# The up products of a gated MLP by Strassen's seven block products, with the residual kept in DRAM

## The chip, the cores and the metric

The kernel runs on one core of one Trainium2 chip. The metric is the device time of one execution in microseconds (us). A core has TensorE (PE in the profile; its weight loads are PEld), VectorE (DVE), ScalarE (ACT), GpSimd (POOL) and SyncE (SP), which here issues nearly all DMA transfers. On-chip memory is SBUF, with 128 partitions; matmuls write to PSUM, eight banks of 128 x 512 float32.

## The reference

Two decoder layers over 1024 tokens of width 1024: first a gated DeltaNet mixer, then sliding-window attention. After the mixer each layer has a gated MLP with a causal depthwise convolution, then a small gated embedding; one RMSNorm closes. The change concerns the MLP:

```python
def conv_ffn(x, w_up, conv_w, w_down):          # D_FF = 2816, three taps
    u = causal_dwconv(x @ w_up, conv_w)         # x: 1024 tokens x 1024
    gate, val = u[..., :D_FF], u[..., D_FF:]
    return (jax.nn.silu(gate) * val) @ w_down

h = h + mix
h = h + conv_ffn(rmsnorm(h, norm_ffn[i]), f_w_up[i], f_conv[i], f_w_down[i])
```

## The kernel before

Channels lie on the partitions and tokens along the free axis, so that a tile is 128 channels x 1024 tokens. Every float32 product is made of three passes: an operand is split into a high part in the matmul's own format (fp32r) and a low part, the rest; high by high, high by low and low by high are added up in PSUM. Weights come from DRAM tile by tile (`load_w`: the DMA, the high part on ACT at line 192, the low part on POOL at line 193). Activations are split once, the high part on ACT and the low part on DVE (lines 236 and 237, with the norm's weight multiplied in).

The mixer's output projection ends in `OutProj.finish`: per tile of the residual `hT[m]` 18 matmuls, two additions from PSUM (line 837), then `Norm.add`, which splits the tile and adds its square to a running sum (lines 255, 256). The norm's factor for a token is multiplied in later, on the way out of PSUM.

The MLP (`ffn`) has 22 pairs of a gate tile and a value tile. `up(j)` makes both: two weight tiles, each by all eight channel tiles and both halves of the tokens, 2 x 2 x 8 x 3 = 96 matmuls of 512 columns. Each half leaves PSUM by one DVE multiplication (line 292). The convolution is one ACT pass (line 295) and two DVE passes (line 297) for a tile. Then come silu on ACT, gate times value on DVE (line 1133), and the split of the product, ACT and POOL (lines 231, 232). `down` multiplies two to four finished pairs at a time into all eight residual tiles and adds 16 PSUM halves to `hT`, which stays in SBUF (line 1166); for one pair this is 48 matmuls on average. So one pair costs TensorE 144 matmuls of 512 columns.

What sets the order: a scheduler places each engine's instructions by its own estimates, and each engine then runs its list strictly in that order. In parts where `E.pinned` is set, TensorE keeps the order in which the program is written; in the MLP it is not set before, and is set after. Buffers are fixed tiles: 40 slots of 4 KB per partition (`Slots`, reused oldest first), weight buffers in rings (`wraw`, `whi`, `wlo`, three of each), and PSUM rings `mm` (3 banks), `d` (3) and `s` (2). Waits arise where a ring or slot is not yet free.

Of the kernel before, what the change touches and what calls it, by code (L numbers as in the profile page):

```python
# [8 lines left out]
F32 = mybir.dt.float32  # L9
# [29 lines left out]
# matmul passes of the running product put between the steps of a chain:  # L39
# DeltaNet's decay, its heads' preparation, inverses, scan, the last scan; attention  # L40
# [7 lines left out]
GROUPS = [2, 4, 4, 4, 4, 4]  # L48


class Slots:
    """Hands out the fixed 4 KB tiles; a tile given back is reused oldest first."""
# [6 lines left out]
    def get(self, name, dt=F32, w=T):  # L59
        self.free.sort()  # L60
        i = self.free.pop(0)[1]
        self.n += 1
        t = self.pool.tile([P, w], dt, tag=f"S{i}", name=f"{name}_{self.n}")
        return Slot(t, i)

    def put(self, *ts):
        for t in ts:
            self.free.append((self.n, t.i))

# [33 lines left out]
def kernel(  # L103
# [36 lines left out]
    class PE:  # L140
        """TensorE; while pinned is set its instructions keep the order they are written in"""
# [54 lines left out]
    def passes(ps, wh, wl, xs, h, k0=0):  # L196
        """a product's matmuls, one a step"""
# [18 lines left out]
    def proj(src, xs, bank=None):  # L216
        """[128 outputs, T] in two PSUM tiles."""
# [8 lines left out]
    def split(t, name, scale=None, eng=V, parts=1):  # L226
        """float32 tile -> two float32r tiles whose sum it is (times scale)."""
# [13 lines left out]
    class Norm:  # L241
        """RMSNorm over channels, tile by tile: the weight goes onto the
        tiles, the per-token factor comes as a row tile at the end."""
# [32 lines left out]
        def rows(self):  # L276
            """the factor along the tokens, on every partition"""
# [4 lines left out]

    def spread(dst, r):
        """a column of each 128 tokens -> a row on every partition"""
# [3 lines left out]
        A.copy(dst, pb)  # L288
# [11 lines left out]
    def delta_layer():  # L300
# [21 lines left out]
        # TensorE is warm by the time the first tile is there  # L322
# [76 lines left out]
        # a chunk's matrix takes P more than its P * P elements, so that the  # L399
# [418 lines left out]
    class OutProj:  # L818
# [36 lines left out]
        def finish(self, nxt):  # L855
# [6 lines left out]
            for a, b in xs:  # L862
                S.put(a, b)
# [528 lines left out]
```

## Time and profile before

| | us |
|---|---|
| time, median of 3 runs | 2845.87 |
| the runs | 2845.24 to 2848.56 |
| span of the profiled execution | 2841.9 |
| PE busy | 2757.3 (97%) |
| DVE busy | 1362.0 (48%) |
| ACT busy | 940.2 (33%) |
| POOL busy | 944.9 (33%) |
| MLP of layer 0, by its first and last adds | about 743 to 1480 |
| MLP of layer 1 | about 1972 to 2716 |

The span runs from the first to the last instruction on the core. The page gives no time of its own for the profiled execution; the median lies 3.97 us above its span. Busy shares are means over stages of different kinds, and a busy matmul is counted from its issue to the end of its pipeline, so neighbours overlap. The rows used below are in a section of their own.

### The profile page before, as it was taken

Reading aid. Unit: us, or ns where it says so; the run is one execution under the profiler, and the core shown is the slowest. Engines: PE = TensorE matmul, PEld = TensorE weight load, DVE = VectorE, ACT = ScalarE, POOL = GpSimd, SP = SyncE. Lnnn points to the kernel's source line nnn. Section 1 sums busy time; section 2 is a strip of 40 time slices with the busy share of each in tenths; the row PEclk is TensorE's granted clock in tenths of the full one; section 3 lists DMA queues with packets and bytes.
Section 4 is the critical chain, followed back from the end, with each engine's and each line's share of the span. In section 5 each row is a group of like instructions: output and inputs, shape, how many; then the busy total and the mean of one; then the engine's idle time right before and its main releaser. Section 6 shows DMA issues by size and latency. Waiting matters only on the chain. (4 is left out here: it accounts for less than half of the span.)

```text
span 2841.9 us, 33819 instructions
## 1 busy us (share of the span) xinstructions
PE 2757.3 (97%) x13442; PEld 2233.0 (79%) x13442; DVE 1362.0 (48%) x1885; ACT 940.2 (33%) x1696; POOL 944.9 (33%) x850
## 2 busy tenths in 40 slices
PE   8999999999999999999999998999999999999998
PEld 7777887878888888888878776678888888888786
DVE  6455455564644343434354346654542434343555
ACT  5333343342422121212243235643321212121343
POOL 4444343341332333223232322222323322323344
PEclk9999999999999999999999999999999999999998
DMA  4222121231120211111112211221111020111123
GB/s 160 86 70 70 55 68 48 57 108 47 54 63 27 65 30 66 30 64 35 58 58 77 88 56 42 54 68 61 44 44 60 30 67 27 63 30 60 51 88 107
DMA packets 111758, 172.95 MB, mean 61 GB/s; under 512 B 32752, under 2 KB 68976, under 8 KB 111600
## 3 DMA queue, kind: packets, MB, share of 16 engines
q1 hardware_dynamic: 110736, 169.41, 19.3%
q8 instruction: 106, 1.74, 0.2%
q10 hardware_dynamic: 864, 1.38, 0.1%
q14 instruction: 52, 0.43, 0.0%
HBM read 148.67 MB, written 15.79 MB: 58 GB/s over the span
## 5 line engine op out<-in xcount | busy, mean ns | idle before, releaser
L193 POOL TENSOR_TENSOR wlo<-wraw,whi 128x1024 fp32r<-128x1024 f32 (+4 forms) x306 | 567.6, 1856 | 1197.2 <-ACT whi L192 1175.0
L146 PE MATMUL mm<-xh,whi 128*128 128x512 f32 x1560 | 634.9, 407 | 1.1 <-DVE gt L292 1.0
L146 PE MATMUL mm<-xh,wlo 128*128 128x512 f32 x1560 | 626.6, 402 | 1.0 <-POOL wlo L193 0.9
L146 PE MATMUL mm<-xl,whi 128*128 128x512 f32 x1560 | 623.5, 400 | 2.4 <-DVE xl L237 2.4
L192 ACT CAST whi<-wraw 128x1024 fp32r<-128x1024 f32 (+4 forms) x306 | 247.1, 808 | 1013.2 <-PE d L146 766.9
L146 PEld LDWEIGHTS mm<-xh,wlo 128*128 128x128 f32 x1560 | 295.6, 189 | 67.0 <-POOL wlo L193 1.8
L146 PEld LDWEIGHTS mm<-xl,whi 128*128 128x128 f32 x1560 | 295.8, 190 | 60.6 <-DVE xl L237 3.6
L146 PEld LDWEIGHTS mm<-xh,whi 128*128 128x128 f32 x1560 | 295.5, 189 | 58.2 <-issue 2.2
L297 DVE SCALAR_TENSOR_TENSOR yf<-zf,fcv,yf 128x1024 f32<-128x1024 f32 x176 | 284.2, 1618 | 109.4 <-ACT yf L295 106.5
L146 PE MATMUL d<-xh,whi 128*128 128x512 f32 x808 | 319.2, 395 | 0.0
L146 PE MATMUL d<-xh,wlo 128*128 128x512 f32 x808 | 319.0, 395 | 0.0
L146 PE MATMUL d<-xl,whi 128*128 128x512 f32 x808 | 318.7, 394 | 0.0
L292 DVE TENSOR_TENSOR zf<-d,rb 128x512 f32<-128x512 f32 x88 | 60.9, 692 | 373.1 <-PE d L146 373.1
L146 PEld LDWEIGHTS d<-xh,wlo 128*128 128x128 f32 x808 | 151.9, 188 | 36.4
L146 PEld LDWEIGHTS d<-xl,whi 128*128 128x128 f32 x808 | 151.6, 188 | 36.4
L146 PEld LDWEIGHTS d<-xh,whi 128*128 128x128 f32 x808 | 151.7, 188 | 35.6
L146 PE MATMUL mm<-gh,wlo 128*128 128x512 f32 x352 | 138.8, 394 | 3.1 <-POOL wlo L193 3.1
L232 POOL TENSOR_TENSOR gl<-yf,gh 128x1024 fp32r<-128x1024 f32 x44 | 105.8, 2404 | 104.6 <-ACT gh L231 104.4
L146 PE MATMUL mm<-gh,whi 128*128 128x512 f32 x352 | 138.7, 394 | 0.0
L146 PE MATMUL mm<-gl,whi 128*128 128x512 f32 x352 | 138.7, 394 | 0.0
L146 PE MATMUL d<-gh,wlo 128*128 128x512 f32 x352 | 138.6, 394 | 0.0
L146 PE MATMUL d<-gl,whi 128*128 128x512 f32 x352 | 138.5, 394 | 0.0
(291 smaller groups left out, 4113.5 us busy)
## 6 DMA issues: line engine op xcount, KB each, us to landing
wraw<-f_up SPq DMA_DIRECT2D x88, 512.0 KB, 3.4
wraw<-f_down SPq DMA_DIRECT2D x80, 256.0 KB, 2.6
wraw<-a_in SPq DMA_DIRECT2D x32, 512.0 KB, 3.5
wraw<-g_w SPq DMA_DIRECT2D x24, 512.0 KB, 3.4
row<-rowd SPq DMA_DIRECT2D x16, 512.0 KB, 4.3
wraw<-b_in SPq DMA_DIRECT2D x12, 512.0 KB, 3.6
ad<-A SPq DMA_DIRECT2D x8, 512.0 KB, 3.2
X<-xd SPq DMA_DIRECT2D x8, 512.0 KB, 4.4
```

What stands on the lines that cost most here:

```text
L146: i = nc.tensor.matmul(*a, **k)
L192: A.copy(hi, raw)
L193: G.tensor_tensor(lo, raw, hi[:, :].bitcast(F32), SUB)
L232: eng.tensor_tensor(lo[:, :], t[:, 0:T], hi.f(), SUB)
L292: V.tensor_tensor(dst[:, off + h * 512:off + (h + 1) * 512], ps2[h], rb[:, hs(h)], MUL)
L297: V.scalar_tensor_tensor(dst[:, 0:T], z[:, i:i + T], w[:, i:i + 1], dst[:, 0:T], MUL, ADD)
```

## The change

Strassen's scheme (in Winograd's form). Rows of the block matrix are gate and value, the inner dimension is split into even and odd channel tiles, and the tokens into their two halves. Seven block products of 4 x 3 = 12 matmuls take the place of eight: 84 matmuls instead of 96 for a pair. For this

- the activations become seven sets, `b11`, `b21`, `b22` (blocks as they are) and `t1` to `t4` (sums of blocks), each in high and low parts. They are made by `Mix.add`, tile by tile, at the end of the mixer's output projection, in place of `Norm.add`;
- three further sums and one more of the weight blocks are made on DVE for each pair (`weights`), and all seven weight blocks are split in pieces of 512 columns, four products ahead (`AHEAD`);
- the products are combined on DVE on their way out of PSUM; three banks (`p1`, `p7`, `p5`) take two products each. The norm's factors stay in the two `s` banks. Nine DVE instructions of 512 columns take the place of four;
- the residual `h` goes to DRAM (`hf`) and is read and written again for each `step` of the down products. A step is one output tile by two pairs, 12 matmuls; up to four steps stand between the up products of a pair. Before, a down product took four pairs for most groups. The last four pairs are taken as before, with `h` loaded back;
- the split of gate times value has its low part on DVE instead of POOL; convolution inputs use two fixed tiles (`S.wide`) instead of slots.

```diff
 class OutProj
-        def finish(self, nxt):
+        def finish(self, nxt, l):
             xs = self.parts(NP1, KT)
-            nrm = Norm(nxt)
-            fx = []
+            mix = Mix(nxt, l)
             for m in range(KT):
                 self.add(m, xs, NP1)
-                fx.append(nrm.add(self.h[m]))
...
+                mix.add(m, self.h[m])
+            return mix
+    class Mix:
...
+        def pair(self, t, name, names, eng):
...
+            for h in range(2):
+                A.copy(hi[:, hs(h)], t[:, hs(h)])
+                eng.tensor_tensor(lo[:, hs(h)], t[:, hs(h)], hi[:, hs(h)].bitcast(F32), SUB)
...
+        def add(self, m, t):
+            nc.sync.dma_start(self.hf[m], t[:, 0:T])
+            xw = S.get("xw")
+            for h in range(2):
+                A.activation(xw[:, hs(h)], t[:, hs(h)], AF.Copy, scale=self.nrm.w[:, m:m + 1])
+            a, b = hs(0), hs(1)
+            if m % 2 == 0:
+                self.t12 = S.get("t12")
+                V.tensor_tensor(self.t12[:, a], xw[:, a], xw[:, b], SUB)
+                bb = S.get("b11", F32R)
+                A.copy(bb[:, a], xw[:, a])
+                V.tensor_tensor(bb[:, b], xw[:, a], bb[:, a].bitcast(F32), SUB)
...
+            else:
+                t12, x0 = self.t12, self.xw
+                V.tensor_tensor(t12[:, b], xw[:, b], t12[:, a], ADD)
+                self.pair(t12, "t12", ("t1", "t2"), V)
+                t34 = S.get("t34")
+                V.tensor_tensor(t34[:, a], x0[:, b], xw[:, b], SUB)
+                V.tensor_tensor(t34[:, b], xw[:, a], t12[:, b], SUB)
+                S.put(t12, x0)
+                self.pair(t34, "t34", ("t3", "t4"), G)
+                S.put(t34)
+                self.pair(xw, "x1", ("b21", "b22"), G)
+                S.put(xw)
+            self.nrm.square(t)
+            S.put(t)
...
+        def halves(src):
...
+            A.copy(hi, src)
+            G.tensor_tensor(lo, src, hi.bitcast(F32), SUB)
+            return hi, lo
...
+        def weights():
...
+                yield halves(a11)
+                V.tensor_tensor(s1, a21, a22, ADD)
+                V.tensor_tensor(s2, s1, a11, ADD)
+                yield halves(s2)
+                V.tensor_tensor(s3, a11, a21, ADD)
+                yield halves(s3)
+                yield halves(s1)
+                yield halves(a12)
+                yield halves(a22)
+                V.tensor_tensor(s2, s2, a12, ADD)
...
+                yield halves(s2)
...
+        def load_step():
...
+            nc.sync.dma_start(w, f_down[l, m, :, a * P:(a + 2) * P])
...
+            nc.sync.dma_start(t[:, 0:T], hf[m])
+            A.copy(hi, w)
+            G.tensor_tensor(lo, w, hi[:, :].bitcast(F32), SUB)
...
+        def step():
+            a, m, hi, lo, t = loaded.pop(0)
+            load_step()
+            xs = [gs[a], gs[a + 1]]
+            for h in range(2):
+                ps = pdt()
+                mm3(ps, hi, lo, xs, h)
+                V.tensor_tensor(t[:, hs(h)], t[:, hs(h)], ps, ADD)
+            nc.sync.dma_start(hf[m], t[:, 0:T])
...
+        def up(j, early, late):
...
+            if j == 0:
+                w = take(4)
+                ps = [pmt(), pdt(), pmt(), pmt()]
+                for k in range(KT // 2):
+                    for p, v, xn in zip(ps, w, ("b11", "t2", "t3", "t1")):
+                        prod(p, v, xn, (k,))
...
+            else:
+                p1 = pmt()
+                prod(p1, *take(), "b11")
+                A.copy(dd, p1)
+                for _ in range(early[0]):
+                    step()
+                p6 = pdt()
+                prod(p6, *take(), "t2")
+                V.tensor_tensor(dd, p6, dd, SUB)
+                for _ in range(early[1]):
+                    step()
+                gated(j - 1)
+                p7 = pmt()
+                prod(p7, *take(), "t3")
+                V.tensor_tensor(zh(z2, 1), p7, dd, ADD)
+                p5 = pmt()
+                prod(p5, *take(), "t1")
+                V.tensor_tensor(zh(z2, 1), zh(z2, 1), p5, SUB)
+                V.tensor_tensor(zh(z2, 1), zh(z2, 1), rb[1], MUL)
...
+            prod(p1, *take(), "b21", first=False)
...
+                A.copy(zh(z1, 0), p1)
+                V.tensor_tensor(zh(z1, 0), zh(z1, 0), rb[0], MUL)
+                prod(p7, *take(), "t4", first=False)
...
+            V.tensor_tensor(zh(z2, 0), p7, dd, ADD)
+            V.tensor_tensor(zh(z2, 0), zh(z2, 0), rb[0], MUL)
+            for _ in range(late[0]):
+                step()
+            ys[j] = taps(2 * j + 1, z2)
+            prod(p5, *take(), "b22", first=False)
...
+            V.tensor_tensor(zh(z1, 1), p5, dd, SUB)
+            V.tensor_tensor(zh(z1, 1), zh(z1, 1), rb[1], MUL)
+            for _ in range(late[1]):
+                step()
```

The scheduler's order shows in three places. First TensorE where the MLP of layer 0 begins. Before, the first two products take the eight split tiles (`xh`, `xl`) in turn:

```order
L146 MATMUL mm<-xh_6032,whi 128x512
L146 MATMUL mm<-xl_6033,whi 128x512
L146 MATMUL mm<-xh_6032,wlo 128x512
L146 MATMUL d<-xh_5789,whi 128x512
L146 MATMUL d<-xl_5790,whi 128x512
L146 MATMUL d<-xh_5789,wlo 128x512
```

After, the last matmul of the output projection (`oh`, `ol`) is followed by the first four products in turn, three matmuls each (`b` is `b11`, the first `t12h` is `t2`, `t34h` is `t3`, the second `t12h` is `t1`):

```order
L152 MATMUL mm<-oh_5756,wlo 128x512
L152 MATMUL mm<-b_197_5796,whi 128x512 x2
L152 MATMUL mm<-b_197_5796,wlo 128x512
L152 MATMUL d<-t12h_5833,whi 128x512
L152 MATMUL d<-t12l_5834,whi 128x512
L152 MATMUL d<-t12h_5833,wlo 128x512
L152 MATMUL mm<-t34h_5842,whi 128x512
L152 MATMUL mm<-t34l_5843,whi 128x512
L152 MATMUL mm<-t34h_5842,wlo 128x512
L152 MATMUL mm<-t12h_5833,whi 128x512
```

So the fourth matmul of the MLP already needs the weights of a second block.

Second, POOL at the same place. Before, it has only the low parts of weights there (128x384 for the output projection):

```order
L193 TENSOR_TENSOR wlo<-wraw,whi 128x640
L193 TENSOR_TENSOR wlo<-wraw,whi 128x384 x2
L779 TENSOR_TENSOR f<-f,mhalf 128x8
L193 TENSOR_TENSOR wlo<-wraw,whi 128x384
L1125 MEMSET zf_6179 128x2
L193 TENSOR_TENSOR wlo<-wraw,whi 128x384 x4
```

After, the low parts of `b21` and `b22` (`x1l`) and of `t3` and `t4` (`t34l`) stand between them, and the low parts of the summed weights (from `sa`, `sb`) behind them:

```order
L199 TENSOR_TENSOR wlo<-wraw,whi 128x384 x2
L898 TENSOR_TENSOR x1l_5946<-xw_5926,x1h_5945 128x512 x2
L898 TENSOR_TENSOR t34l_5940<-t_214_5936,t34h_5939 128x512 x2
L199 TENSOR_TENSOR wlo<-wraw,whi 128x384 x2
L898 TENSOR_TENSOR x1l_6043<-xw_6023,x1h_6042 128x512
L1193 TENSOR_TENSOR wlo<-wraw,whi 128x512
L898 TENSOR_TENSOR x1l_6043<-xw_6023,x1h_6042 128x512
L898 TENSOR_TENSOR t34l_6037<-t_227_6033,t34h_6036 128x512 x2
L898 TENSOR_TENSOR x1l_6140<-xw_6120,x1h_6139 128x512 x2
L898 TENSOR_TENSOR t34l_6134<-t_240_6130,t34h_6133 128x512 x2
L1193 TENSOR_TENSOR wlo<-sa_6148,whi 128x512 x2
L1193 TENSOR_TENSOR wlo<-sb_6149,whi 128x512
```

Sixteen subtractions of 512 columns have come in, and the low parts that the second and third product of the MLP need are behind the last of them.

Third, DVE in the middle of the MLP. Before, a pair's convolution (`yf`) and its product come between evacuations (`zf`) and additions to `h`:

```order
L292 TENSOR_TENSOR zf_7167<-mm,rb_6166 128x512
L292 TENSOR_TENSOR zf_7167<-d,rb_6166 128x512
L297 SCALAR_TENSOR_TENSOR yf_7171<-zf_7167,fcv,yf_7171 128x1024
L1166 TENSOR_TENSOR h_5058<-h_5058,mm 128x512
L297 SCALAR_TENSOR_TENSOR yf_7171<-zf_7167,fcv,yf_7171 128x1024
L1133 TENSOR_TENSOR yf_7107<-yf_7107,yf_7171 128x1024
L1166 TENSOR_TENSOR h_5058<-h_5058,d 128x512
```

After, sums of weights (`sa`, `sb` from `wraw`), combinations (`zv`, `zg`, `sb` from `d`), additions to `h` and the two passes of a convolution are interleaved:

```order
L1297 TENSOR_TENSOR h_8300<-h_8300,d 128x512 x2
L1211 TENSOR_TENSOR sa_6148<-wraw 128x512
L1214 TENSOR_TENSOR sb_6149<-wraw 128x512
L1297 TENSOR_TENSOR h_8345<-h_8345,d 128x512 x2
L1330 TENSOR_TENSOR sb_6149<-d,sb_6149 128x512
L1212 TENSOR_TENSOR sa_6148<-sa_6148,wraw 128x512
L1297 TENSOR_TENSOR h_8388<-h_8388,d 128x512 x2
L309 SCALAR_TENSOR_TENSOR yf_8450<-zg_6150,fcv,yf_8450 128x1024 x2
L1336 TENSOR_TENSOR zv_6151<-mm,sb_6149 128x512
L1267 TENSOR_TENSOR yf_8450<-yf_8450,yf_8321 128x1024
L1339 TENSOR_TENSOR zv_6151<-zv_6151,mm 128x512
L1340 TENSOR_TENSOR zv_6151<-zv_6151,s 128x512
```

An addition that frees a `d` bank now has convolution passes and sums of weights ahead of it in DVE's list. Over the program the list of matmuls loses 528 of 512 columns, and DVE's has 606 instructions more.

## Rows read from the trace of the kernel before

**Rows 1.** The page's busy times: engine, busy us and share, instructions.

```profile
PE 2757.3 (97%) x13442; PEld 2233.0 (79%) x13442; DVE 1362.0 (48%) x1885; ACT 940.2 (33%) x1696; POOL 944.9 (33%) x850
```

**Rows 2.** Stretches: start:end, us, busy us by engine, granted clock, DMA share, GB/s.

```profile
712.00:770.00 58.00, 58.00 (x264) 47.20 (x263) 33.81 (x38) 27.25 (x31) 20.32 (x16) 1.00 0.19 64
830.00:1400.00 570.00, 570.00 (x2455) 460.66 (x2454) 223.64 (x222) 130.59 (x136) 171.77 (x120) 1.00 0.16 48
...
1400.00:1480.00 80.00, 78.44 (x338) 63.17 (x337) 42.87 (x43) 32.49 (x35) 28.63 (x16) 1.00 0.16 50
...
2660.00:2716.00 56.00, 54.46 (x244) 44.13 (x243) 34.38 (x37) 26.55 (x31) 19.70 (x12) 1.00 0.19 59
```

**Rows 3.** PE's waits from 712 to 1490: us in total, times, longest.

```profile
PE mm L146 <- POOL wlo L193: 1.6, 1, 1.6
```

**Rows 4.** DVE, ACT, POOL by line and shape: busy us, mean ns, idle before.

```profile
L1133 DVE TENSOR_TENSOR yf<-yf,yf 128x1024 f32<-128x1024 f32 x44 | 53.9, 1224 | 1.4
L297 DVE SCALAR_TENSOR_TENSOR yf<-zf,fcv,yf 128x1024 f32<-128x1024 f32 x176 | 284.2, 1618 | 109.4 <-ACT yf L295 106.5
L192 ACT CAST whi<-wraw 128x512 fp32r<-128x512 f32 x80 | 49.5, 621 | 319.5 <-PE d L146 318.9 <-issue 0.6
L295 ACT ACTIVATE yf<-zf,fcv 128x1024 f32<-128x1024 f32 x88 | 101.2, 1150 | 15.2 <-DVE zf L292 15.1
L232 POOL TENSOR_TENSOR gl<-yf,gh 128x1024 fp32r<-128x1024 f32 x44 | 105.8, 2404 | 104.6 <-ACT gh L231 104.4
```

**Rows 5.** DVE lines, duration in ns: minimum/median/maximum, first and last start.

```profile
L292 DVE TENSOR_TENSOR zf<-d,rb x88: 680/692/695, 767.6 to 2660.9; 128x512 f32<-128x512 f32 x88
L297 DVE SCALAR_TENSOR_TENSOR yf<-zf,fcv,yf x176: 1277/1285/3548, 769.6 to 2664.2; 128x1024 f32<-128x1024 f32 x176
L256 DVE TENSOR_TENSOR sq<-sq,sqt x42: 1210/1218/3235, 12.8 to 2710.4; 128x1024 f32<-128x1024 f32 x42
L1267 DVE TENSOR_TENSOR sq<-sq,gt x12: 691/2111/2123, 2729.6 to 2820.3; 128x512 f32<-128x512 f32 x12
```

**Rows 6.** DVE in order of time, 2728 to 2734: start us, us.

```profile
2728.18 0.69 DVE L1261 TENSOR_TENSOR h<-h,gt 128x512 f32<-128x512 f32 x1
...
2733.25 1.74 DVE L1261 TENSOR_TENSOR h<-h,gt 128x512 f32<-128x512 f32 x1
```

**Rows 7.** POOL in order of time, 2726 to 2735, same columns.

```profile
2726.35 0.74 POOL L193 TENSOR_TENSOR wlo<-wraw,whi 128x256 fp32r<-128x256 f32 x1 [1.59 <-ACT whi L192]
2732.04 2.40 POOL L193 TENSOR_TENSOR wlo<-wraw,whi 128x1024 fp32r<-128x1024 f32 x1 [4.95 <-ACT whi L192]
```

**Rows 8.** DVE at the end of layer 0's output projection, in order of time.

```profile
712.53 1.29 DVE L837 TENSOR_TENSOR h<-h,mm 128x512 f32<-128x512 f32 x2 [1.07 <-PE mm L146]
...
743.13 0.67 DVE L837 TENSOR_TENSOR h<-h,mm 128x512 f32<-128x512 f32 x1
```

**Rows 9.** POOL beside it, in order of time.

```profile
716.88 1.02 POOL L193 TENSOR_TENSOR wlo<-wraw,whi 128x384 fp32r<-128x384 f32 x1 [2.47 <-ACT whi L192]
...
729.38 1.49 POOL L193 TENSOR_TENSOR wlo<-wraw,whi 128x384 fp32r<-128x384 f32 x1 [2.72 <-ACT whi L192]
```

**Rows 10.** Stretches in which the granted clock is lower, columns as in Rows 2.

```profile
1730.00:1740.00 10.00, 7.18 (x42) 4.76 (x41) 4.58 (x6) 7.08 (x21) 1.28 (x2) 0.74 0.44 107
1740.00:1750.00 10.00, 9.79 (x60) 7.53 (x59) 6.34 (x25) 3.90 (x14) 2.10 (x2) 0.92 0.01 2
...
2830.00:2842.00 12.00, 1.12 (x4) 0.72 (x4) 5.83 (x6) 0.58 (x1) 3.99 (x3) 0.50 0.46 175
```

**Rows 11.** DMA issues: KB each, median us from issue to landing.

```profile
hd<-h SPq DMA_DIRECT2D x8, 512.0 KB, 3.0
h<-hd SPq DMA_DIRECT2D x8, 512.0 KB, 5.4
```

**Rows 12.** A stretch of heavy DMA traffic, columns as in Rows 2.

```profile
10.00:15.00 5.00, 4.15 (x19) 3.05 (x18) 4.00 (x3) 5.00 (x7) 4.60 (x5) 1.00 1.03 419
```

More of the change, by code (lines that the diff above doesn't have):

```diff
@@ L38 @@
 NSLOT = 40
+AHEAD = 4
 FG1, FG2, FG3 = 84, 4, 50
@@ L47 @@
 SLOTW = T + 4
-GROUPS = [2, 4, 4, 4, 4, 4]
+NLAST = 4
 class Slots:
@@ L57, in __init__, with get @@
         self.n = 0
-    def get(self, name, dt=F32, w=T):
+    def get(self, name, dt=F32):
         self.free.sort()
@@ L62, in get @@
         self.n += 1
-        t = self.pool.tile([P, w], dt, tag=f"S{i}", name=f"{name}_{self.n}")
+        t = self.pool.tile([P, T], dt, tag=f"S{i}", name=f"{name}_{self.n}")
         return Slot(t, i)
@@ L68, in put, with wide @@
             self.free.append((self.n, t.i))
+    def wide(self, name):
+        self.n += 1
+        return self.pool.tile([P, SLOTW], F32, tag="Z", name=f"{name}_{self.n}", bufs=2)
 class Slot:
@@ L281, in rows, with banks @@
             return rb
+        def banks(self):
+            return [spread(None, self.r[:, 4 * h:4 * h + 4]) for h in range(2)]
     def spread(dst, r):
@@ L287, in spread @@
             E.transpose(ch(pb, c), r[:, c:c + 1].broadcast_to([P, P]), ident)
-        A.copy(dst, pb)
+        if dst is not None:
+            A.copy(dst, pb)
+        return pb
     def evac(dst, off, ps2, rb):
@@ L440, in act_tile @@
             A.activation(y[:, :], y[:, :], AF.Silu)
-            S.put(z)
             res[key] = y
@@ L1103, in swa_layer @@
         E.pinned = False
[L1104 removed]
+        return op.finish(3, 1)
     fcv = const("fcv", [P, 2 * 2 * NF * CF], f_conv)
[L1109 to L1139 removed]
@@ L1140, in down @@
             fx = []
-            nn = Norm(nxt) if last else None
+            nn = Norm(nxt)
             def load(m):
@@ L1147, in down @@
             early = []
-            for m in range(NEARLY if last else 0):
+            for m in range(NEARLY):
                 wh, wl = load(m)
@@ L1161, in down @@
                         ps = ps2[h]
-                        mm3(ps, wh, wl, gs[-1:], h, k0=n - 1, first=False)
+                        mm3(ps, wh, wl, xs[-1:], h, k0=n - 1, first=False)
                     else:
                         ps = pany()
-                        mm3(ps, wh, wl, gs, h)
+                        mm3(ps, wh, wl, xs, h)
                     V.tensor_tensor(hT[m][:, hs(h)], hT[m][:, hs(h)], ps, ADD)
-                if last:
-                    fx.append(nn.add(hT[m]))
-            for a, b in gs:
+                fx.append(nn.add(hT[m]))
+            for a, b in xs:
                 S.put(a, b)
             return fx, nn
-        pend = None
-        j = 0
-        for n in GROUPS:
-            gs = [up(j)]
-            if pend is not None:
-                down(*pend, False)
-            for i in range(1, n):
-                gs.append(up(j + i))
-            pend = (j, gs)
-            j += n
-        for a, b in xs:
-            S.put(a, b)
-        S.put(state["rb"])
+        for j in range(NF):
+            n = len(todo) + len(loaded)
+            if j == 2:
+                load_step()
+            if j < 2 or n == 0:
+                early = late = (0, 0)
+            elif j == 2:
+                early, late = (0, 0), (1, 1)
+            elif n == 2:
+                early, late = (1, 1), (0, 0)
+            else:
+                early, late = (1, 1), (1, 1)
+            up(j, early, late)
+        S.put(sa, sb)
+        hT = []
+        for m in range(KT):
+            t = S.get("h")
+            nc.sync.dma_start(t[:, 0:T], hf[m])
+            hT.append(t)
+        gated(NF - 1)
+        E.pinned = False
         ps_in = load_p(l)
-        return *down(*pend, True), ps_in
+        j0 = NF - NLAST
+        return hT, *down(j0, [gs.pop(j0 + i) for i in range(NLAST)]), ps_in
     def load_p(l):
@@ L1348, in layout @@
     bt = _tiles(bw)
-    up = np.stack([_tiles(w) for w in i["f_w_up"]])
+    ev = [k * P + c for s in range(2) for k in range(s, KT, 2) for c in range(P)]
+    up = np.stack([_tiles(w[ev]) for w in i["f_w_up"]])
     order = [s * NF + j for j in range(NF) for s in range(2)]
```

164 lines of the change are left out of this document (123 added, 41 removed).

## The prediction

> **What bounds the kernel now.** I read the busy times first: TensorE is at work for 97% of the span and no other engine for half of it [rows 1]. Busy time alone does not prove a bound, so next the stretches. In the middle of layer 0's MLP TensorE is busy for all of 570 us with 2455 matmuls at a granted clock of 1.00, so one matmul of 512 columns takes 570/2455 = 0.2322 us of its time; where the mixer's output projection passes into the MLP (712 to 770) there is no gap either [rows 2]. The waits confirm it: from 712 to 1490 TensorE lost 1.6 us to another engine that the profile can name [rows 3]. The reader is to see that in the MLP a matmul taken away is time taken away, as long as the engines behind TensorE keep pace. DVE works 223.64 of those 570 us and POOL 171.77 [rows 2].
>
> **What goes.** 12 of 144 matmuls for each of 22 pairs in two layers: 528 x 0.2322 = 122.6 us. A pair with four down steps then takes 132 x 0.2322 = 30.65 us instead of 33.4.
>
> **What comes, in the middle of the MLP.** Per pair and engine:
> - DVE: 17 instructions of 512 columns with an operand from PSUM (nine combinations, eight additions to h) at 0.69 [rows 5] are 11.7 us. With both operands in SBUF: four sums of weights at 0.69 (the shortest 512 case of the fourth line), four convolution passes at 1.285 [rows 5], gate times value 1.22 [rows 4] and the low part of its split, taken as 1.22 as well: 10.3 us. Together 22 of 30.65 us, 72%.
> - POOL: a low part of 1024 columns takes 2.40 [rows 4], so 512 take some 1.2, and 256 take 0.74 [rows 7]: 7 x 1.2 + 4 x 0.74 = 11.4 us, 37%.
> - ACT: seven high parts at 0.62, two first taps at 1.15 [rows 4], and copies, silu and small casts of about the same sizes: near 11 us.
> - DMA: two up tiles of 0.5 MB and four steps of 1.15 MB (weights, h in, h out) are 5.6 MB, or 183 GB/s against 48 before [rows 2]. The start of the program ran at 419 GB/s with the queues full [rows 12], so these are below half loaded.
>
> No engine is over its time. But DVE and POOL are in each other's way. A DVE instruction that needs 0.69 took 1.74 when POOL's subtraction, begun at 2732.04 and 2.40 long, was under way; it ended 0.55 after POOL did [rows 6, 7]. The convolution passes have a median of 1.285 and a mean of 1.618 [rows 4, 5], while those fed from PSUM stay between 680 and 695 ns [rows 5]. POOL is held likewise: 1.49 for what takes 1.02 [rows 9]. I scale that: before, 5 exposed DVE instructions per pair met a POOL busy 30% of the time and lost 4 x 0.333 = 1.3 us; after, ten meet one busy 37% of the time, in pieces half as long: about 2 us. DVE is then at 24 of 30.65 us.
>
> Does TensorE notice? The `d` ring of three banks is the tightest: in the two early steps a bank is wanted again 18 matmuls, 4.2 us, after it was filled, and DVE's list has a convolution (2.6 us), gate times value and a sum or two ahead of that addition, which need 5 to 6 us but were ready some 2 us earlier. So it fits with about a microsecond to spare, for every second pair; the others have their convolution after these additions. I take 0.3 us lost per pair over 36 pairs with steps, 11 us; bounds 0 and 1 us per pair, 0 to 36. In each layer's first two pairs and its last there are no steps, and a pair lasts 84 x 0.2322 = 19.5 us, with 10.3 + 8.4 = 18.7 us of work that DVE and POOL can't do at once: 3 us lost per layer, 6 in all (0 to 14).
>
> **What comes, at the seam.** Here the change moves work to the worst place. In the 30.6 us between the projection's first and last additions to h [rows 8] DVE and POOL must now make seven sets of activations. Work that DVE and POOL can't do at once, up to the second product's low part: on DVE 28 sums and low parts at 0.69, seven additions of squares at 1.22 [rows 5] and two sums of weights, 29.2 us; on POOL 16 low parts at 1.2, six of the projection's weights at 1.02 [rows 9] and three of the up weights at 1.2, 28.9 us. Together 58.1 us. The first of it can start at about 715 (the additions of 712.53, then two ACT passes of 0.62), so it ends at 773, or 2 us earlier because DVE instructions in a row overlap a little (1.29 for two) [rows 8]. POOL's list puts the low parts of the summed weights behind the last activations, and TensorE has only the three matmuls of `b11` before it needs them. It is through with the projection at about 743.1 and with these at 743.8: 27 us lost per layer. From below: if the two engines never met, DVE's 29.2 us and 16 additions at 0.69 end at 752.7, and the casts and POOL's four last low parts 6 us later: 15 us. From above: 2.5 us more for each of four pairs of tiles in which DVE waits for ACT's passes: some 39. I take 27, near the sum because the rows show the blocking; two layers, 54 (30 to 78).
>
> A rule of the Trainium skill speaks to this: its page "SBUF — State Buffer", section "SBUF: two separate sides", says that DVE instructions with two SBUF inputs and GpSimd's instructions take one pair of ports in turn, as an exclusive lock for the whole instruction. By that rule the seam's whole 58.1 us are serial and each layer loses 27 to 29; without it 15. The trace agrees with the lock (1.74 for 0.69, above).
>
> After such a gap the granted clock will be lower for a while: in 1730 to 1740, with TensorE busy for 7.18 of 10 us, it was 0.74, in the next 10 us 0.92, and at the end, with TensorE nearly idle, 0.50 [rows 10]. At most 2.6 + 0.8 = 3.4 us; I take 2 per layer, 4 (0 to 7).
>
> **What else goes.** At the MLP's end TensorE idled 1.56 and 1.54 us [rows 2] while the last pair's two tiles were convolved and split; now only the gate's is left by then, and the low part is on DVE instead of POOL (1.22 for 2.40). The 54 matmuls of other pairs that are put before it last 12.5 us and cover about 10 of chain: 3 us gained. The h tiles are read back in that time (8 x 0.5 MB).
>
> **Sum.** Against the span: 2841.9 - 122.6 + 54 + 4 + 11 + 6 - 3 = 2791.3. The median of the runs is 4.0 us above the span, so 2795 us.
>
> **The rivals.**
> 1. The seam hardly costs: the scheduler's order lets POOL's and DVE's pieces fit into each other's pauses. The lower seam (30) and no losses in the middle: 2841.9 - 122.6 + 30 - 3 + 4 = 2750. For it: the old seam had no gap, though DVE was busy for 33.81 and POOL for 20.32 of its 58 us [rows 2]. Against: the new one has twice the work that they can't share.
> 2. Traffic of h: a step's h tile takes a slot that an earlier tile has just left for DRAM, so a load waits for a store. Before, a store took 3.0 us and a load 5.4 [rows 11], and SP's list is served in order. If that costs 1 us for each pair, 2795 - 11 + 36 = 2820. Against: a load is issued 13 us or more before its use.
> 3. Slower than before: DVE becomes the bound. If every POOL piece blocks DVE in full, DVE needs 22 + 11.4 = 33.4 us per pair, and its waits for ACT in list order (first tap, silu, high part) come on top, at least one of 1.15: 34.6, which is 4 us over TensorE's 30.65. Then 36 x 4 = 144 and the time is 2795 - 11 + 144 = 2928. It decides the sign from 62 / 36 = 1.7 us lost per pair. For it: DVE's list is strict, one late addition holds up all others. Against: the measured blocking before was 1.3 us per pair, not 10.
> 4. The gain is only a shorter list: something else in the MLP sets the pace at the old 33.4 us per pair, and the seam's cost stays: about 2850. The unbroken PE row speaks against it.
>
> **How the numbers follow.** My forecast has 0.62, and its own range is 2770 to 2820. Rival 1 has 0.17, rival 2 has 0.10, rival 3 has 0.08, rival 4 has 0.03. Less than 0.2% (5.7 us) can't be told from no change here. Faster then is the forecast and the first two, 0.89 less a little for their upper ends: 0.87; rival 4 and those ends give the same 0.04; slower 0.09. The range 2748 to 2840 takes in rivals 1 and 2 and leaves rival 3 and 4 out.
>
> **What would show it.** Right: PE's waits at the two seams name POOL's low parts (`wlo`, `t34l`) or DVE, with gaps of 20 to 30 us each near 745 and 1935; the stretches in the middle show 132 matmuls per 31 us at clock 1.00, with PE busy above 98%; convolution passes of median 1.285 and maxima down from 3.5 to about 2.5. Wrong: seams without a gap (rival 1); PE waiting in the middle for DVE's additions to h by more than 1 us per pair (rival 3), or ACT and DVE waiting for DMA of h (rival 2); a pitch of matmuls other than 0.232 where PE is busy, which would make the first term false.

## The result, and the profile after

The changed kernel takes 2816.8 us (median of 4 runs, 2807.2 to 2819.0) where the kernel before took 2845.6 in the same comparison: a ratio of 0.9893, with a 95% interval of 0.9874 to 0.9911. The forecast was 2795 within 2748 to 2840, faster. Of the 122.6 us of matmuls taken away 28 arrived, by the spans of the two profiles; 72 were expected to be lost, some 94 were. The profiled execution has a span of 2813.8 us.

Two marks that both programs have divide the span: DVE's first addition of the second part of each output projection (its line is 837 before and 848 after), and TensorE's first `d<-pl` matmul behind each MLP. The third column is a second profile of the kernel before, the last the best kernel of the experiments (five edits with 4112-byte slots). Stages that the change leaves alone differ by a few us from run to run: the first between 709.9 and 716.8 in the fourteen profiles, the third between 443 and 452.

| us | before | before, again | after | best |
|---|---|---|---|---|
| DeltaNet, to the first mark | 712.5 | 710.9 | 714.0 | 709.9 |
| layer 0: end of projection, MLP | 771.1 | 771.1 | 753.7 | 725.5 |
| to the next mark (attention) | 451.6 | 451.8 | 451.5 | 448.7 |
| layer 1: end of projection, MLP | 782.1 | 782.1 | 769.3 | 734.9 |
| rest | 124.6 | 124.3 | 125.2 | 123.7 |

So layer 0 gained 17.4 and layer 1 12.8 of 61.3 us each. The stretches that answer to those of [rows 2] (start:end, us, busy us and instructions of PE, PEld, DVE, ACT, POOL, granted clock, DMA share, GB/s):

```profile
712.00:770.00 58.00, 35.29 (x139) 25.67 (x137) 53.55 (x55) 38.99 (x62) 38.88 (x24) 0.86 0.33 116
830.00:1400.00 570.00, 561.96 (x2399) 449.63 (x2399) 412.95 (x495) 198.16 (x311) 266.69 (x202) 1.00 0.53 181
1400.00:1480.00 80.00, 78.09 (x328) 62.17 (x327) 51.75 (x53) 35.56 (x42) 26.22 (x18) 0.98 0.34 112
```

The seam lost 22.7 us of TensorE's 58, and DVE, at 33.81 before, is now busy for 53.55 of them. The middle is 98.6% full. POOL is busy there for 47% of the time, where 37% was forecast, and DVE for the 72% that was forecast without any blocking. TensorE's waits from 712 to 1490, which were 1.6 us before [rows 3] (us, times, longest):

```profile
PE d L152 <- ACT whi L1192: 12.3, 1, 12.3
PE d L152 <- DVE h L1297: 8.0, 8, 1.8
PE mm L152 <- DVE h L848: 6.1, 3, 3.5
PE mm L152 <- POOL wlo L199: 2.2, 2, 1.1
PE mm L152 <- ACT gh L237: 1.8, 1, 1.8
```

The largest is one wait for the high part of the second product's weights; the second is the steps' additions to h; the third the additions inside the projection. TensorE at the seam, in order of time (start, us, [idle before and releaser]):

```profile
750.22 0.40 PE L152 MATMUL mm<-oh,wlo 128*128 128x512 f32 x1
754.15 1.16 PE L152 MATMUL mm<-b,whi 128*128 128x512 f32 x2 [3.53 <-DVE h L848]
755.11 0.63 PE L152 MATMUL mm<-b,wlo 128*128 128x512 f32 x1
768.02 0.79 PE L152 MATMUL d<-t12h,whi 128*128 128x512 f32 x1 [12.29 <-ACT whi L1192]
...
770.18 0.79 PE L152 MATMUL d<-t12h,wlo 128*128 128x512 f32 x1 [0.93 <-POOL wlo L1193]
...
771.20 0.63 PE L152 MATMUL mm<-t34l,whi 128*128 128x512 f32 x1
771.62 0.63 PE L152 MATMUL mm<-t34h,wlo 128*128 128x512 f32 x1
```

After these waits the last two start 0.42 us apart instead of 0.233: that is the lower of TensorE's two clock levels (1.2 instead of 2.4 GHz), and from 760 to 790 the granted clock is 0.76.

What it waited for, on DVE and then on POOL:

```profile
765.58 1.74 DVE L1212 TENSOR_TENSOR sa<-sa,wraw 128x512 f32<-128x512 f32 x1
767.24 1.75 DVE L1214 TENSOR_TENSOR sb<-wraw 128x512 f32<-128x512 f32 x1
```

```profile
762.97 3.80 POOL L898 TENSOR_TENSOR t34l<-t,t34h 128x512 fp32r<-128x512 f32 x2 [1.28 <-ACT t34h L897]
766.74 3.39 POOL L1193 TENSOR_TENSOR wlo<-sa,whi 128x512 fp32r<-128x512 f32 x2
```

The sum `s2` (L1212) is a 0.69 us instruction that took 1.74 beside POOL's low part, and it stands in DVE's list behind the last activations. In the middle the convolution passes have the median forecast, 1.285, with maxima of 1.73 and 3.29 where about 2.5 was forecast (minimum/median/maximum in ns, first and last start):

```profile
L309 DVE SCALAR_TENSOR_TENSOR yf<-zv,fcv,yf x88: 1269/1284/1728, 794.2 to 2630.3; 128x1024 f32<-128x1024 f32 x88
L309 DVE SCALAR_TENSOR_TENSOR yf<-zg,fcv,yf x88: 1268/1285/3294, 799.5 to 2637.2; 128x1024 f32<-128x1024 f32 x88
```

The gate's is the one that is held up, and it stands ahead of late additions. One such place, on ACT, DVE, POOL and TensorE:

```profile
1279.16 1.15 ACT L307 ACTIVATE yf<-zg,fcv 128x1024 f32<-128x1024 f32 x1 [3.18 <-DMA hf<-h]
```

```profile
1280.35 3.52 DVE L309 SCALAR_TENSOR_TENSOR yf<-zg,fcv,yf 128x1024 f32<-128x1024 f32 x2 [1.92 <-ACT yf L307]
1283.79 0.67 DVE L1297 TENSOR_TENSOR h<-h,d 128x512 f32<-128x512 f32 x1
```

```profile
1280.90 1.89 POOL L1193 TENSOR_TENSOR wlo<-wraw,whi 128x512 fp32r<-128x512 f32 x1 [4.10 <-ACT whi L1192]
1282.74 2.27 POOL L1193 TENSOR_TENSOR wlo<-sa,whi 128x512 fp32r<-128x512 f32 x1
```

```profile
1288.07 0.50 PE L152 MATMUL d<-gh,dhi 128*128 128x512 f32 x1 [1.82 <-DVE h L1297]
```

The convolution's tile has a slot that an h tile has just left, so its first tap waits 3.18 us for that tile's store (17.5 us in nine places from 830 to 1400). Its two DVE passes then run beside POOL's low parts (3.52 us instead of some 2.5), and the additions behind them come 1.8 us late for TensorE.

### The profile page after: what moved, and what is told of

Same layout as the page of the kernel before. It is cut to its first block, busy times and chain, and to the rows that moved or that the text cites. A ratio compares the mean times of both kernels' runs of the same rounds, so it can differ in the third digit from the quotient of the medians.

```text
span 2813.8 us, 35193 instructions
## 1 busy us (share of the span) xinstructions
PE 2669.6 (95%) x12914; PEld 2144.8 (76%) x12914; DVE 1799.4 (64%) x2491; ACT 1108.4 (39%) x2134; POOL 1177.4 (42%) x1038
## 5 line engine op out<-in xcount | busy, mean ns | idle before, releaser
L199 POOL TENSOR_TENSOR wlo<-wraw,whi 128x1024 fp32r<-128x1024 f32 (+4 forms) x138 | 260.6, 1891 | 455.3 <-ACT whi L198 421.0
L152 PE MATMUL mm<-xh,whi 128*128 128x512 f32 x856 | 357.7, 418 | 1.1 <-DVE gt L304 1.0
L152 PE MATMUL mm<-xh,wlo 128*128 128x512 f32 x856 | 349.7, 409 | 0.9 <-POOL wlo L199 0.8
L152 PE MATMUL mm<-xl,whi 128*128 128x512 f32 x856 | 346.4, 405 | 2.5 <-DVE xl L243 2.5
L1193 POOL TENSOR_TENSOR wlo<-sa,whi 128x512 fp32r<-128x512 f32 x132 | 197.5, 1497 | 169.7 <-ACT whi L1192 169.6
L1193 POOL TENSOR_TENSOR wlo<-wraw,whi 128x512 fp32r<-128x512 f32 x132 | 194.6, 1481 | 138.8 <-ACT whi L1192 138.8
L152 PE MATMUL d<-gh,dhi 128*128 128x512 f32 x576 | 229.7, 399 | 12.1 <-DVE h L1297 12.1
L152 PE MATMUL d<-gh,dlo 128*128 128x512 f32 x576 | 227.8, 396 | 0.0
L152 PE MATMUL d<-gl,dhi 128*128 128x512 f32 x576 | 227.8, 395 | 0.0
L1297 DVE TENSOR_TENSOR h<-h,d 128x512 f32<-128x512 f32 x288 | 193.8, 682 | 32.2 <-PE d L152 31.4
L152 PEld LDWEIGHTS mm<-xh,whi 128*128 128x128 f32 x856 | 163.6, 191 | 27.9 <-issue 2.0
```

The costliest lines, as they stand in the source:

```text
L152: i = nc.tensor.matmul(*a, **k)
L199: G.tensor_tensor(lo, raw, hi[:, :].bitcast(F32), SUB)
L1193: G.tensor_tensor(lo, src, hi.bitcast(F32), SUB)
L1297: V.tensor_tensor(t[:, hs(h)], t[:, hs(h)], ps, ADD)
```

## The experiments

All ratios are to the kernel before on the same chip in the same comparison. The changed kernel is at 0.9893.

### Low parts of the activations on DVE: 0.9848 (0.9832 to 0.9865), 2798.0 us

```
- self.pair(t34, "t34", ("t3", "t4"), G)
+ self.pair(t34, "t34", ("t3", "t4"), V)
- self.pair(xw, "x1", ("b21", "b22"), G)
+ self.pair(xw, "x1", ("b21", "b22"), V)
```

> The 16 low parts per seam of t3, t4, b21 and b22 are made by DVE instead of POOL, nothing else. Theory A (what ends the seam is work that DVE and POOL can only do one after the other): the serial sum falls by 16 x (1.2 - 0.69) = 8 us per seam and DVE's 1.75 us instructions go back to 0.69, so TensorE's wait for the second product's weights gets some 8 us shorter in each layer and the kernel about 16 us faster than the changed one (about 2801). Theory B (DVE's own list is the bound, POOL's blocking matters little): DVE gets 16 x 0.6 = 10 us more per seam, so about 20 us slower (2837).

Theory A: some 13 us by the ratio, where 16 were expected. DVE ran 72 instructions instead of 55 in the same 58 us and was busy for less of them, 48.45 instead of 53.55:

```profile
712.00:770.00 58.00, 38.63 (x147) 29.04 (x146) 48.45 (x72) 39.09 (x64) 17.14 (x10) 0.86 0.36 119
```

The two layers took 745.0 and 762.1, together 15.9 us less. The wait for the weights only fell from 12.3 to 10.1 us: the place of the weights in the list is a cost of its own.

### The first weights ahead of the last two tiles: 0.9805 (0.9783 to 0.9826), 2785.1 us

```
  for m in range(KT):
      self.add(m, xs, NP1)
      ...
+         mix.up = up_weights(l)          # m == KT - 1: two tiles, three sums, four sets
+         mix.add(m - 1, self.h[m - 1])
+     if m != KT - 2:
          mix.add(m, self.h[m])
```

> The first four sets of up weights of each layer (two tiles loaded, three sums, four high and low parts) are written in the program before the activations of the last two h tiles instead of behind all of them; the sum of the work is the same. Theory A (the place in the lists decides: TensorE waits for the second product's weights while the activations of six of eight tiles lie ready): TensorE does 36 of the first 48 matmuls, 8.4 us, while the last two tiles are converted, and runs them at the full clock: 8 to 11 us per layer, about 18 us faster than the changed kernel (2799). Theory B (the last activations end the seam, and the weights only happen to be named): the last twelve matmuls start as late as before, and the gain is only the 36 matmuls that no longer follow, or less where DVE is held up by the sums: 0 to 8 us in all (2809 to 2817).

Theory A, and more than it asked for: layer 0 takes 743.1 and layer 1 752.0, 27.9 us less together, 25 by the ratio. TensorE's waits from 712 to 790:

```profile
PE mm L152 <- DVE h L911: 4.6, 3, 2.0
PE d L152 <- POOL wlo L845: 3.5, 1, 3.5
PE d L152 <- ACT whi L844: 2.8, 1, 2.8
```

The one wait of 12.3 us has become 3.5 and 2.8, and the matmuls of six tiles run while the last two are converted.

### Sums of squares on TensorE: 0.9876 (0.9856 to 0.9897), 2804.7 us

```
- V.tensor_tensor(self.sq, self.sq, tmp, ADD)
+ for c in range(NCH):
+     E.matmul(self.ps[:, c:c + 1], ch(tmp, c), ones[:, 0:1], start=self.k == 0, stop=self.k == KT - 1)
```

The factors that this kernel computes are not the reference's, so it serves for its time alone.

> The sums of squares at the two seams are accumulated by TensorE in a PSUM bank (eight matmuls with one column for each h tile) instead of seven additions of 1024 columns on DVE. If DVE's list sets the end of the seam, it loses 7 x 1.22 to 2.3 us, some 9 to 12 us per seam, while TensorE gets 56 x 0.107 = 6 us more, most of it where it waits anyway: 5 to 10 us per layer, about 15 us faster than the changed kernel (2802). If POOL's low parts or ACT's casts set the end, nothing is gained and TensorE's 6 us are paid: about 8 us slower (2825).

Inconclusive: 0.0017 better than the changed kernel, with intervals that overlap. The wait of 12.3 us for the weights is gone (2.7 for POOL and 5.0 for the squares are left). `s2` is done at 764.0 instead of 767.3, so a shorter list of DVE brings the weights earlier; but TensorE also comes to the first product only at 771.1 instead of 754.2, so how much of the wait DVE's list had set isn't shown. I had priced a product at 0.107 us and missed that the records count each of these float32 matmuls twice:

```profile
L152 PE MATMUL s<-ones,sqt x256: 164/250/371, 718.5 to 1970.1; 128*128 128x1 f32 x128
```

The program's 128 matmuls (64 per layer) have 256 records, and those of layer 0's seam took 17 us of TensorE; the eight of the changed kernel take 1.7. What DVE gave, TensorE paid.

### Slots that don't wait for stores: 0.987 (0.9847 to 0.9894), 2805.1 us

```
+ if name in ("yf", "gh", "gl"):   # the oldest free slot that no stored h tile has left
+     k = next((k for k, (n, i) in enumerate(self.free) if i not in self.stored), 0)
+ elif name == "h":                # the oldest that one has left
+     k = next((k for k, (n, i) in enumerate(self.free) if i in self.stored), 0)
```

> Only the choice of the free 4 KB slot differs: tiles of the convolution and the gate's split take a slot that does not come from an h tile whose store may still be under way, and h tiles take such slots. Theory A (in the middle of the MLP the gate's convolution starts late because its slot waits for a store of h; it then meets POOL's two low parts of weights, and DVE's next addition comes 2 us late): ACT's wait of some 3 us for hf<-h goes, the steps' waits of TensorE for DVE's additions (12.1 us in eleven places) nearly vanish, 8 to 12 us faster than the changed kernel (2806). Theory B (only the two engines' blocking makes the additions late): the waits stay, no change (2817).

Theory A in part, and by the trace; by the ratio alone it isn't shown, since the intervals overlap. The first taps' waits for `hf<-h` are gone from 830 to 1400, and of TensorE's 8.0 us of waits for additions there 3.0 are left:

```profile
PE d L159 <- DVE h L1304: 3.0, 2, 1.8
```

From 880 to 1400 TensorE is busy for 519.87 us of 520, against 514.31 in the changed kernel. In the middle of layer 1, though, 3.1 of 4.0 us are left. In both layers together half of the 12.0 us is gone; they were to vanish nearly all.

### Low parts of the up weights on DVE: 0.9801 (0.9781 to 0.9821), 2785.8 us

```
- G.tensor_tensor(lo, src, hi.bitcast(F32), SUB)     # halves()
+ V.tensor_tensor(lo, src, hi.bitcast(F32), SUB)
```

> The changed kernel with the low parts of the up weights (seven of 512 columns a pair) on DVE instead of POOL, at the seams and in the middle. DVE then has some 29 of the 30.8 us of a pair by the durations without blocking, POOL only the four of 256. Theory A (blocking is what makes DVE late; without POOL's long pieces its convolution passes are all at 1.285 and nothing meets them): TensorE's 12 us of waits for additions in the middle go or stay as small as they are, and each seam gets some 5 us shorter: about 10 us faster than the changed kernel, 0.986. Theory B (DVE is near its bound, the third rival of the prediction): its additions come late in every pair by 1 us or more, 36 us or more slower, 1.00 or above.

Theory A, at more than twice the size I gave it. From 880 to 1400 in the changed kernel, and then in this one:

```profile
880.00:1400.00 520.00, 514.31 (x2197) 411.83 (x2196) 377.07 (x450) 182.05 (x284) 241.27 (x183) 1.00 0.53 181
```

```profile
880.00:1400.00 520.00, 520.00 (x2230) 418.64 (x2229) 430.90 (x576) 187.21 (x290) 64.10 (x66) 1.00 0.54 184
```

POOL gave away 177 us of work and DVE's busy time rose by 54. DVE's 120 low parts at 0.686 are 82 us, so 28 us of stretched instructions went with POOL's pieces:

```profile
L1193 DVE TENSOR_TENSOR wlo<-sa,whi x52: 681/685/1234, 881.0 to 1397.8; 128x512 fp32r<-128x512 f32 x52
L309 DVE SCALAR_TENSOR_TENSOR yf<-zg,fcv,yf x36: 1275/1285/1289, 886.0 to 1396.6; 128x1024 f32<-128x1024 f32 x36
```

TensorE waits for nothing there, nor in the middle of layer 1, with DVE at 83%; the first taps still wait for `hf<-h` (15.2 us in eleven places). The third rival's ground, a DVE near its bound, is not where the loss was.

### Three edits together: 0.9776 (0.9760 to 0.9793), 2780.5 us

Activations' low parts on DVE, weights first, slots.

> The three edits that were faster alone, together: low parts of the activations on DVE, the first four sets of weights ahead of the last two tiles, and slots that don't wait for stores. Alone they moved the ratio to the kernel before from 0.9893 to 0.9848, 0.9805 and 0.987. Theory A (three causes that add up: blocking, order, slots): 0.9893 - 0.0045 - 0.0088 - 0.0023 = 0.974, about 2766 where the kernel before takes 2840. Theory B (the first two are the same wait at the seam, counted twice): 0.978, about 2778.

Theory B: little of the first edit's gain is left beside the second. In the projection TensorE still waits 9.7 us (layer 0) for DVE's additions, since three banks fill up.

### Activations behind the next projection, six banks, four late squares: 0.9784 (0.9766 to 0.9801), 2783.7 us

```
- ps2 = proj(..., xs)
+ ps2 = proj(..., xs, pany)
- mix.add(m, self.h[m])            # behind add(m)
+ mix.add(m - 1, self.h[m - 1])    # behind add(m)
```

> As the three edits together, and at the seam three things more: each h tile's activations are written behind the next tile's projection, the projection's products take all six banks instead of three, and the last four additions of squares come behind the first products' weights. If DVE's list still sets the end of the seam, its 4 x 1.22 us and TensorE's waits for additions inside the projection (7 us in layer 0 and 12 in layer 1 of the changed kernel) go: 8 to 14 us faster than the three together, 0.970. If the last tile's casts and low parts end it whatever comes before, the projection is only done sooner and TensorE waits longer behind it: the same as the three together.

No gain, as the second of the two expectations has it. The projection's waits for DVE are gone, and TensorE waits behind it instead, from 712 to 800:

```profile
PE d L160 <- ACT whi L859: 8.4, 1, 8.4
PE d L160 <- POOL wlo L860: 6.4, 1, 6.4
```

The three edits went in at once, so which of them brought these waits isn't told apart.

### Five edits: 0.9705 (0.9686 to 0.9723), 2760.2 us; with 4112-byte slots 0.9667 (0.9652 to 0.9681), 2747.9 us

Low parts of activations and of up weights on DVE, weights first, slots, six banks. The second has one more edit:

```
- t = self.pool.tile([P, T], dt, tag=f"S{i}", ...)
+ t = self.pool.tile([P, SLOTW], dt, tag=f"S{i}", ...)    # used as t[:, 0:T]
```

> The three edits that were faster (low parts of the activations on DVE, first weights ahead of the last two tiles, slots that don't wait for stores) and two more: the low parts of the up weights on DVE too, and the projection's products in six banks instead of three. In the run with the three, TensorE still lost some 26 us per layer in the 85 us around each seam and at the layer's end: 10 us in waits for additions inside the projection (three banks), some 6 in matmuls at the lower clock behind them, 3 in two early additions. Theory A (POOL's pieces are what stretches DVE's list, and the banks turn its delay into TensorE's): both go, 8 to 15 us per layer less one or two for the low parts that DVE now makes itself: 0.970, about 2758 where the kernel before takes 2843. Theory B (DVE's own list is the bound at the seam): nine more low parts of 0.69 there cost what the blocking gave, and six banks only move the wait behind the projection: 0.977.

> As the run beside it (five edits), with one difference in the layout of SBUF: slots are 4112 bytes apart, as in the kernel before, instead of 4096; instructions and their order are the same. The kernel before showed 0.2325 us from matmul to matmul on two chips, the changed kernel and all its variants 0.2333. Theory A (the addresses do it: in the kernel before tiles of activations start at two different offsets within 64 bytes): the distance falls below 0.2333 and the time by up to 0.3%, 4 to 8 us. Theory B (the order of instructions or the traffic does it): still 0.2333 and no difference between the two.

Theory A in both; the layout was worth 12 us, more than the 4 to 8 expected. In the first the layers take 731.3 and 741.2, in the second 725.5 and 734.9. DVE at the seam, second kernel:

```profile
744.37 0.68 DVE L918 TENSOR_TENSOR h<-h,mm 128x512 f32<-128x512 f32 x1
744.96 0.68 DVE L918 TENSOR_TENSOR h<-h,d 128x512 f32<-128x512 f32 x1
...
746.76 0.68 DVE L852 TENSOR_TENSOR wlo<-wraw,whi 128x512 fp32r<-128x512 f32 x1
747.36 0.68 DVE L870 TENSOR_TENSOR sa<-wraw 128x512 f32<-128x512 f32 x1
```

With POOL out of the way nothing is stretched. TensorE's waits from 709 to 1440 begin with the first product's low part, which stands behind these additions:

```profile
PE mm L159 <- DVE wlo L852: 8.2, 1, 8.2
PE d L159 <- ACT whi L851: 1.8, 1, 1.8
PE mm L159 <- ACT gh L244: 1.7, 1, 1.7
```

### The same, with two additions of squares later: 0.9683 (0.9661 to 0.9705), 2753.5 us

```
- self.nrm.square(t)
+ self.nrm.square(t, m >= 6)    # these are added behind the first products' weights
```

> As the five edits with the 4112-byte slots, and the additions of squares of the last two h tiles at each seam come behind the first products' weights in the program. DVE works without a pause through the seam (0.68 us after 0.68), and TensorE waits 8.4 and 8.8 us for the first product's low part in its list. If DVE's list is the bound to the end of the seam, 2 x 1.22 us less in it are worth up to 2.4 us per layer, some 4 us in all (2744, ratio 0.9655). If TensorE's start on the first product decides, which lies ahead of both additions in the list, nothing (2748).

No gain: the wait for the first low part is still 8.3 us in layer 0 and 8.6 in layer 1 (8.2 and 8.6 without the edit), and TensorE now waits 1.6 us per layer for the late additions themselves.

### The kernel before once more, and the changed kernel with the other layout

> The kernel before, unchanged, profiled once more on another chip. In its first profile matmuls of 512 columns follow each other every 0.2325 us on average where TensorE is busy (it varies from 0.2314 to 0.2329), in the changed kernel and in the four experiments so far every 0.2333. If that difference belongs to one execution or one chip, this profile shows 0.2333, and the unchanged stages (451.6 us for the attention layer, 124.6 for the end) are some 0.3% longer against their neighbours; if it belongs to the kernel, it shows 0.2325 again.

> The changed kernel with the layout alone altered: slots 4112 bytes apart, as in the kernel before; instructions and order are the same. With the five edits this took the distance between matmuls from 0.2333 to 0.2318 us and 12 us off the time. Theory A (the layout is a cost of its own, which the change brought along): the distance falls below 0.2330 here too, every stage that TensorE fills gets shorter, the 714.0 us before the first seam among them, and the kernel takes some 8 to 12 us less than the changed one (2816.8): about 2806, ratio 0.986. Theory B (the gain came from another meeting of the five edits with the layout): no difference, 0.9893.

The kernel before showed 0.2324 again on another chip (2841.9 us, one run). The changed kernel with 4112-byte slots took 2802.2 us, 0.9862 (0.9839 to 0.9885), and its matmuls follow each other every 0.2319 us instead of 0.2333 (means over stretches of 28 us in the MLPs). Its layers are 3.5 and 7.5 us shorter; the stage before the first seam, which was to get shorter too, is not (715.3 us). 4112 bytes is the width of the tiles; where they lie in SBUF stands in no trace. With slots of 4096 bytes a matmul's record has nearly one length; with 4112 it varies and is a little shorter in the median. The `d<-pl` matmuls (ns) of the kernel before in its second profile, of the changed kernel, and of the changed kernel with 4112-byte slots:

```profile
L146 PE MATMUL d<-pl,whi x44: 387/394/399, 1481.9 to 2822.9; 128*128 128x512 f32 x44
```

```profile
L152 PE MATMUL d<-pl,whi x44: 395/396/396, 1467.8 to 2795.9; 128*128 128x512 f32 x44
```

```profile
L152 PE MATMUL d<-pl,whi x44: 390/394/399, 1465.6 to 2783.2; 128*128 128x512 f32 x44
```

The changed kernel's interval with 4112-byte slots overlaps the one without. But the five edits with and without them ran on one chip, in the same order of instructions, with intervals just apart, and the time from matmul to matmul falls in both pairs: the layout costs by itself, which is shown. Why it does is open.

## Why the prediction was right, and where it was off

The direction, the mechanism and the range held; the sum was 22.5 us too low. The time lies nearer to the second rival's 2820 than to the forecast, but that rival has 36 us lost in the middle beside the 6 of the first and last pairs, and the middle lost 17.7 in all. Here are the prediction's own terms, from the trace of after. A loss is a stretch's time less its matmuls of 512 columns at 0.2333 us and its one-column ones; the stretches are 714 to 784 and 1919 to 1994 (seams), 784 to 1415 and 1994 to 2630 (middle), and what follows to the first `d<-pl`. For the ends the 3.4 us of before are taken off. The first row is the forecast's own; the row on a matmul's time is what is left of the layers' times, and not measured by itself:

| term, us | forecast | measured |
|---|---|---|
| 528 matmuls | -122.6 | -122.6 |
| the two seams, with the clock | +58 | +63.3 (28.1 and 35.2) |
| the middle and the first and last pairs | +17 | +17.7 |
| the MLP's ends | -3 | +5.6 |
| a matmul's time | 0 | +5.8 in the layers |
| other stages | 0 | +2.0 |

- **The matmuls.** 264 per layer went, and the middle runs at clock 1.00, 98.6% busy. The time of 0.2322 us from matmul to matmul was taken for a constant. It depends on the layout: before, a slot that ever held a padded tile was 4112 bytes wide; the change gives the padded tiles two places of their own (`S.wide`), and all slots are 4096. The prediction named another pitch as what would make its first term false; it was, by 0.5%. The list of the change names the edit, and I read it as free.
- **The seams.** 58.1 us of work that can't be shared was to end at 771 to 773; in layer 0 POOL's low parts from `sa`, that of `s2` among them, are done at 770.1, and the seam lost 28.1 us, clock included, where 29 were taken. The waits name ACT's high part, DVE and POOL's low parts, in pieces inside and behind the projection (the longest 12.3) and not as one gap of 20 to 30. By kind the term is off both ways: the waits are 22.9 and 26.7 us, 49.6 against 54, and matmuls at the lower clock (more than 0.3 us from start to start without a wait) cost 3.4 and 7.2, 10.6 against 4 (0 to 7); some 3 are the first matmul behind each wait. That the two nearly make up for each other is luck. The clock's term was read from one short gap; at the seam several waits follow each other, and the clock is 0.76 in 760 to 790 and 0.65 in 1980 to 1994. Both halves of the cause are shown: less of POOL's work beside DVE (the activations' low parts on DVE) and another order (the first weights ahead) each shorten it. Layer 1 lost 7 more, with 12.2 us of waits for additions inside the projection instead of 6.1; about half of the 7 is the lower clock. I had taken the layers as equal, and why they differ is open.
- **The lock.** The Trainium skill's page "SBUF — State Buffer", section "SBUF: two separate sides", has DVE instructions with two SBUF inputs and GpSimd's take one pair of ports in turn. These runs agree: 1.74 us for 0.69 beside POOL, 0.68 one after the other without. By that rule work moved from POOL to DVE, which does a low part in 0.69 instead of 1.3, relieves DVE. I had the rule and the rows and still counted POOL's 11.4 us a pair as costing DVE only 2, because 72% and 37% both fit.
- **The middle.** The size was right (12.0 us of waits for additions against the 11 taken) and one reason missing, so the size is in part luck; the other 6, put on the pairs without steps, are matmuls behind the waits, most of them at the lower clock. The second rival, a slot that waits for a store, is there, but where I didn't look: not at the loads of h, but at the gate's convolution, which starts late and then meets POOL's low parts. Taking away the slots' waits ends half of the late additions, taking away POOL's low parts of up weights all of them.
- **The MLP's ends.** This term failed, by 8.6 us, and from its first step. I read the 1.56 and 1.54 us of before as the convolution and the split of the last pair. The line in [rows 3] names something else, the low part of a weight tile (line 193):

```profile
1460.09 0.50 PE L146 MATMUL mm<-gh,wlo 128*128 128x512 f32 x1 [1.55 <-POOL wlo L193]
```

  The change doesn't take that work away: in the two runs with the first weights ahead and with the other slots TensorE waits 1.5 us for it again at the end of layer 0. In the changed kernel the wait is for `gh`, 1.8 and 2.8 us, then 0.5 for `gl`, with 2.0 us of matmuls at the lower clock behind each. The 10 us of chain that I had set against the cover of 12.5 left out the next stage: in ACT's list the cast of a tile of the embedding, which waits for its load, stands ahead of the gate's first tap, and the two passes run beside POOL's low part of that tile (2.40 us from 1423.68).

```profile
1422.55 1.05 ACT L237 CAST ph<-p 128x1024 fp32r<-128x1024 f32 x1 [4.03 <-DMA p<-pT]
1423.51 1.15 ACT L307 ACTIVATE yf<-zg,fcv 128x1024 f32<-128x1024 f32 x1
```

```profile
1424.68 3.80 DVE L309 SCALAR_TENSOR_TENSOR yf<-zg,fcv,yf 128x1024 f32<-128x1024 f32 x2 [2.52 <-ACT yf L307]
```

  No run takes these two away alone; in the best kernel no cast stands there in layer 0, and 1.7 us of wait for `gh` are left.
- **The fourth rival.** Its 2850 doesn't follow: with the 122.6 us not gained, the seam's cost kept and the middle's 17 left out, 2795 becomes some 2900. It lies outside the range either way, and the middle at 98.6% with 0.2333 us from matmul to matmul rules it out.

## What to carry to other kernels

Where two engines block each other, add their work up before asking which is fuller: moving the up weights' low parts from the slower to the busier engine was worth 0.9%, with the busier at 83%. At a seam the order of the lists counts as much as the work: what the next stage needs first goes ahead of the last tiles of this one, which alone was worth 25 us. Before an edit of a pool's tiles is costed at nothing, compare the time from matmul to matmul before and after it: the matmuls of 512 columns, 9,680 here, all feel it.

## What the runs showed of the hardware that was not expected

The time from matmul to matmul depends on the layout of the tiles in SBUF: 0.2333 us with all slots 4096 bytes wide, 0.2319 with 4112, at clock 1.00, with the same instructions in the same order; 12 us of 2760.
